# First loads on two queues, sixteen small stack copies and a re-ordered end in a two-layer attention trunk

## The chip, the cores and the metric

The kernel runs on one core of one Trainium2 chip. The metric is device time in microseconds (us) of one execution. The core has TensorE (PE), VectorE (DVE), ScalarE (ACT), GpSimd (POOL) and SyncE (SP); SP, ACT and POOL can issue DMA transfers, each on a queue of its own, in the order of their instructions.

## The reference

The input `x` has 512 tokens of width D = 2048. Two layers follow each other. Each layer is a root-mean-square norm with a gain, one input projection 2048 to 2048 (eight parts of 256), two groups of four attention heads (layer 0: dilated window and block-sparse; layer 1, heads C and D: differential and stick-breaking), a SiLU gate on each, one output projection 512 to 2048, and a residual sum. A final norm with its own gain ends it.

```python
for layer in range(DEPTH):
    h = _rmsnorm(x, norm_g[layer])
    proj = jnp.einsum('bsd,de->bse', h, w_in[layer])
    parts = jnp.split(proj, N_IN_PARTS, axis=-1)
    ...
    y = jnp.concatenate([_merge(o1) * jax.nn.silu(g1), _merge(o2) * jax.nn.silu(g2)], axis=-1)
    x = x + jnp.einsum('bse,ed->bsd', y.astype(x.dtype), w_out[layer])
return _rmsnorm(x, final_norm_g)
```

## The kernel before, in words

**Numbers in two parts.** Every operand is split into a high and a low part (`HH` and `HL`, `YH` and `YL`, `whi` and `wlo`), and a product is made of three matmuls: high by high, high by low, low by high (`mm3`). Activations are kept transposed: 16 blocks `kt` (or `dc` on the output side) of 128 channels by 512 tokens. `x` is transposed on the host.

**Weights.** Both layers' weights are 80 units of 128 x 1024 words, 512 KB each, in the order in which they are used. `load_unit` loads the next one (three `raw` buffers). `split_half` makes `whi` on ScalarE and `wlo` on VectorE or GpSimd for half a unit. `tick` is called before each half unit is used; it loads and splits ahead. All these loads are issued by SP.

**Start.** `run` clears a tile and lets PE run `WARM` products of zeros. SP then issues `xg` (block 0 of `x` and the three gains in one tensor of 560 columns), the two halves of unit 0, block 1 of `x`, unit 1, and blocks 2 to 4. In `layer` for layer 0, `make_h` multiplies a block by its gain (`HH`) and forms the rest (`HL`); for block 0 it does so on VectorE straight from `xg`. `v_unit_half` then runs the four token blocks of the value projection for one `kt`; for the first half unit it runs all four with `HH` and `whi`, then with `HL`, then with `wlo`.

**The order of the middle** is written by hand: `SCHED` gives for each step of the heads a place in PE's stream of 48 or 64 half units, and `layer` calls the steps at these places. `stack4` prepares the queries and the keys of the differential heads: it splits them into `hi` and `lo` and copies them by DMA into `st`, four blocks of 32 partitions, in which each of the four rows holds either the high or the low part. SP and POOL issue four copies each of 64 KB, and POOL then one or two more that copy rows within `st` and so wait until the first have landed. Line 446 multiplies queries by keys.

**Output projection.** `open_dc` takes a bank of the accumulator for block `dc`, and `part` adds one of the four pairs of heads. `PRE` blocks (2 in layer 0, 5 in layer 1) are begun before the last pair of heads is ready; `outproj` adds that pair, the blocks behind them are run at once. The banks are two named `acc` (in layer 1 three named `s` for blocks 2 to 4). `get_x` loads the residual block three steps ahead, in layer 1 into one of four buffers `prob`.

**End.** Layer 1 computes tokens 0 to 383 transposed, like the rest. For the last 128 tokens (`nat`, the natural layout) `last` computes the output projection in units of 256 columns, with sums of squares along the rows. For the transposed part the sums come from `nat_stats`, `replicate` spreads the norm factors over the partitions, and `scale_t` scales each block, which SP writes out. `nat_evac` adds the residual and squares a piece, `nat_sum` adds up the sums, and behind the last piece a short chain makes the last factor, with which VectorE and ScalarE scale all pieces. Before, the gain of the final norm is multiplied into each transposed block by ScalarE in `after`.

## Time and profile before

| | |
|---|---|
| time, median of 3 runs | 527.46 us (527.19 to 529.7) |
| time of the profiled execution | 527.0 us |
| its span, from the first to the last instruction | 524.9 us |
| PE busy | 511.5 us, 97% of the span |
| DVE busy | 331.8 us, 63% |
| ACT busy | 293.3 us, 56% |
| POOL busy | 180.0 us, 34% |

The profile is one execution. Its rows give the start of an instruction or of a run of equal ones, its duration, its engine and line, what it writes and reads, and in brackets how long the engine was idle before it and which engine's work ended that idle time. Matmuls are pipelined: the distance from one start to the next says what one costs, and the duration of a row is longer than that.

### The profile page before, as it was taken

The numbers are of one execution on the slowest core, as the hardware profiler recorded it, in microseconds if no ns is written. First come the engines' busy times: TensorE is split into PE (matmuls) and PEld (weight loads), VectorE is DVE, ScalarE is ACT, GpSimd is POOL, SyncE is SP. The second block draws the span as 40 slices with busy tenths as digits, with TensorE's granted clock in tenths as the row PEclk, the third lists the DMA queues.
The fourth block names the chain that finished last, engine by engine and source line by source line (L and its number), as shares of the span: only waits on it lengthen the run. The fifth ranks groups of instructions, "written<-read, shape, count | busy, mean of one in ns | idle before, by whom it ended". The sixth has DMA issues, their size and how long they took to land.

```text
span 524.9 us, 7398 instructions
## 1 busy us (share of the span) xinstructions
PE 511.5 (97%) x2505; PEld 430.7 (82%) x2505; DVE 331.8 (63%) x678; ACT 293.3 (56%) x588; POOL 180.0 (34%) x171
## 2 busy tenths in 40 slices
PE   8999999999999999999999998999999999999993
PEld 5888888888888888788888887888888888898993
DVE  5545358787786755797862872564557856784444
ACT  5477244355436554566546464743446678857843
POOL 2304353304224023377403233114520322444841
PEclk9999999999999999999999999999999999999998
DMA  8895352244314223688534274232551313156717
GB/s 306 282 401 180 120 124 93 68 117 121 120 41 121 81 80 107 204 288 302 182 121 121 80 200 123 83 119 80 146 145 71 108 54 116 62 179 208 239 70 252
DMA packets 30374, 77.65 MB, mean 148 GB/s; under 512 B 4480, under 2 KB 7424, under 8 KB 29952
## 3 DMA queue, kind: packets, MB, share of 16 engines
q1 hardware_dynamic: 27264, 70.36, 39.3%
q0 software_dynamic: 2784, 6.29, 5.5%
q10 hardware_dynamic: 288, 0.52, 0.3%
q8 instruction: 20, 0.33, 0.3%
q14 instruction: 18, 0.15, 0.1%
HBM read 61.43 MB, written 8.39 MB: 133 GB/s over the span
## 4 chain that ended last, share of the span: by engine, by line
PE 91%; DMA 3%; ACT 2%; DVE 2%; issue 1%; POOL 0%; ACTq 0%; SPq 0%; POOLq 0%
PE acc L187 17%; PE acc L189 17%; PE acc L188 17%; PE oacc L188 5%; PE oacc L189 5%; PE oacc L187 5%; PE v L187 4%; PE v L189 4%; PE v L188 4%; PE ops L509 3%; PE pt L481 3%; PE s L415 2%; DMA st<-st 1%; PE z L532 1%; PE s L446 1%
## 5 line engine op out<-in xcount | busy, mean ns | idle before, releaser
L176 POOL TENSOR_TENSOR wlo<-raw,whi 128x512 fp32r<-128x512 f32 x67 | 90.7, 1359 | 192.3 <-ACT whi L174 146.9
L187 PE MATMUL acc<-hh,whi 128*128 128x512 f32 x384 | 154.2, 402 | 0.0
L189 PE MATMUL acc<-hh,wlo 128*128 128x512 f32 x384 | 150.1, 391 | 0.0
L188 PE MATMUL acc<-hl,whi 128*128 128x512 f32 x384 | 149.7, 390 | 0.0
L174 ACT ACTIVATE whi<-raw 128x512 fp32r<-128x512 f32 x148 | 90.5, 625 | 88.7 <-issue 42.7
L189 PEld LDWEIGHTS acc<-hh,wlo 128*128 128x128 f32 x384 | 72.1, 188 | 15.6
L188 PEld LDWEIGHTS acc<-hl,whi 128*128 128x128 f32 x384 | 72.3, 188 | 12.9
L187 PEld LDWEIGHTS acc<-hh,whi 128*128 128x128 f32 x384 | 72.3, 188 | 12.7
L176 DVE TENSOR_TENSOR wlo<-raw,whi 128x512 fp32r<-128x512 f32 x81 | 59.2, 737 | 29.4 <-ACT whi L174 26.9
L187 PE MATMUL v<-whi,hh 128*128 128x512 f32 x124 | 48.4, 390 | 0.0
L189 PE MATMUL v<-whi,hl 128*128 128x512 f32 x124 | 48.3, 389 | 0.0
L188 PE MATMUL v<-wlo,hh 128*128 128x512 f32 x124 | 48.2, 389 | 0.0
L395 ACT ACTIVATE prob<-prob,m 128x512 f32<-128x512 f32 (+3 forms) x56 | 29.7, 552 | 28.3 <-DVE m L392 28.3
L487 DVE TENSOR_TENSOR pt<-pt 128x384 fp32r<-128x384 f32 (+1 forms) x48 | 27.4, 598 | 22.2 <-ACT pt L486 22.1
L486 ACT ACTIVATE pt<-pt 128x384 fp32r<-128x384 f32 (+1 forms) x48 | 23.5, 524 | 27.2 <-PE pt L481 26.9
L187 PE MATMUL oacc<-y,whi 128*128 128x512 f32 (+1 forms) x80 | 30.9, 386 | 0.1
L188 PE MATMUL oacc<-y,whi 128*128 128x512 f32 (+1 forms) x80 | 30.4, 380 | 0.2 <-DVE y L577 0.2
L189 PE MATMUL oacc<-y,wlo 128*128 128x512 f32 (+1 forms) x80 | 30.3, 378 | 0.0
L189 PEld LDWEIGHTS v<-whi,hl 128*128 128x128 f32 x124 | 23.3, 188 | 4.9
L188 PEld LDWEIGHTS v<-wlo,hh 128*128 128x128 f32 x124 | 23.3, 188 | 4.7
L187 PEld LDWEIGHTS v<-whi,hh 128*128 128x128 f32 x124 | 23.3, 188 | 4.6
L253 POOL TENSOR_TENSOR ss<-ss,sq 128x512 f32<-128x512 f32 x15 | 21.8, 1451 | 11.2 <-ACT sq L249 11.1
(219 smaller groups left out, 836.8 us busy)
## 6 DMA issues: line engine op xcount, KB each, us to landing
raw<-w SPq DMA_DIRECT2D x79, 512.0 KB, 3.4
xr<-xt SPq DMA_DIRECT2D x31, 256.0 KB, 4.4
xnat<-xnat SPq DMA_DIRECT2D x8, 512.0 KB, 7.5
x1d<-x SPq DMA_DIRECT2D x16, 256.0 KB, 2.8
xr<-x1d SPq DMA_DIRECT2D x16, 256.0 KB, 3.5
st<-st POOLq DMA_DIRECT2D x24, 128.0 KB, 3.5
out_t_dram<-x2a SPq DMA_DIRECT2D x10, 192.0 KB, 2.8
out_t_dram<-x2b SPq DMA_DIRECT2D x6, 192.0 KB, 2.5
```

The costliest lines, as they stand in the source:

```text
L174: self.nc.scalar.activation(h, t, AF.Copy)
L176: eng.tensor_tensor(l, t, h.bitcast(F32), op=OP.subtract)
L187: mm(out, lhsT=lh, rhs=rh, start=first, stop=False)
L188: mm(out, lhsT=lh, rhs=rl, start=False, stop=False)
L189: mm(out, lhsT=ll, rhs=rh, start=False, stop=last)
L253: nc.gpsimd.tensor_tensor(ss, ss, sq, op=OP.add)
L395: nc.scalar.activation(p, p, AF.Exp, bias=m[:, t:t + 1], scale=-1.0, **kw)
L415: nc.tensor.matmul(out, lhsT=Q()[:, 2 * i + arr, 128 * t:128 * t + 128], rhs=Q()[:, 4 + i, :n], start=arr == 0, stop=arr == 1)
L481: nc.tensor.transpose(bank[:, col + 128 * (t - c):col + 128 * (t - c) + 128], st["p"][:, QOFF[t] + 128 * c:QOFF[t] + 128 * c + 128], self. ...
L486: nc.scalar.activation(h, src, AF.Copy)
L487: nc.vector.tensor_tensor(l, src, h.bitcast(F32), op=OP.subtract)
L509: nc.tensor.matmul(b[:, 128 * c:], lhsT=self.V[:, c, vh], rhs=st[k][:, OFF[c]:OFF[c] + WID[c]], start=c == 0 and k == "h", stop=c == NT - ...
```

## The change

The first loads are spread over two queues and re-ordered. `xg` holds the first 256 columns of block 0, then the gains, then the other 256 columns, and is loaded in two parts; `make_h0` works on 256 columns at a time. ACT issues the first half of unit 0, and later unit 1, blocks 2 to 4 and unit 2, between its own first steps. The first half unit's products run for token blocks 0 and 1 first, then for 2 and 3. One warm-up product is left out (`WARM` 7).

In `stack4` each row of `st` is copied straight from `hi` or `lo`: eight copies by SP and eight by POOL for 512 columns of each of four blocks, none within `st`.

In the output projection blocks 2 to 4 use the banks `s` in both layers, and for blocks 0 and 1 the two products with `YH` of the last pair of heads run in front of the two with `YL`. In layer 1 the residual blocks are loaded in pairs (`get_pair`), two to a buffer, six ahead.

At the end `replicate` stands in front of the last quarter of unit 1's products, the scaling of block 0 in front of the first piece's evacuation, and the evacuation and sum of the second last piece (`nat_evac(3)`, `nat_sum(3)`) in front of the scalings of blocks 10 and 14. For blocks 0 to 4 the gain is multiplied in `scale_t` on VectorE, and ScalarE's copy in `after` goes.

```diff
@@ -37,7 +37,7 @@
...
 LEAD = [0, 16]
-WARM = 8
+WARM = 7
@@ -139,21 +139,21 @@
...
 
-    def load_unit(self, part=0):
+    def load_unit(self, part=0, eng=None):
...
         if part == 2:
-            self.nc.sync.dma_start(self.raw[0][:, 512:], self.a["w"][0][:, 512:])
+            eng.dma_start(self.raw[0][:, 512:], self.a["w"][0][:, 512:])
...
             self.raw[0] = self.wp.tile([128, 1024], F32, tag="raw", bufs=3, name="raw")
-            self.nc.sync.dma_start(self.raw[0][:, :512], self.a["w"][0][:, :512])
+            eng.dma_start(self.raw[0][:, :512], self.a["w"][0][:, :512])
...
         t = self.wp.tile([128, 1024], F32, tag="raw", bufs=3, name="raw")
-        self.nc.sync.dma_start(t, self.a["w"][u])
+        (eng or self.nc.sync).dma_start(t, self.a["w"][u])
@@ -182,11 +182,17 @@
...
 
-    def mm3(self, out, lh, ll, rh, rl, first, last):
+    def mm3(self, out, lh, ll, rh, rl, first, last, which=3):
         mm = self.nc.tensor.matmul
-        mm(out, lhsT=lh, rhs=rh, start=first, stop=False)
-        mm(out, lhsT=lh, rhs=rl, start=False, stop=False)
-        mm(out, lhsT=ll, rhs=rh, start=False, stop=last)
+        if which == 3:
+            mm(out, lhsT=lh, rhs=rh, start=first, stop=False)
+            mm(out, lhsT=lh, rhs=rl, start=False, stop=False)
+            mm(out, lhsT=ll, rhs=rh, start=False, stop=last)
+        elif which == 2:
+            mm(out, lhsT=lh, rhs=rh, start=first, stop=False)
+            mm(out, lhsT=ll, rhs=rh, start=False, stop=False)
+        else:
+            mm(out, lhsT=lh, rhs=rl, start=False, stop=last)
@@ -231,13 +237,19 @@
...
 
-    def make_h(self, x, l, kt, square=True, g=None):
-        nc = self.nc
-        if g is None:
-            g = self.g[:, l, kt:kt + 1]
-            nc.scalar.activation(self.HH[:, kt], x, AF.Copy, scale=g)
-        else:
-            nc.vector.tensor_scalar(self.HH[:, kt], x, g, None, op0=OP.mult)
+    def make_h0(self, i):
+        nc = self.nc
+        o = i * (S // 2 + 3 * KT)
+        x, g = self.xg[:, o:o + S // 2], self.xg[:, S // 2:S // 2 + 1]
+        w = slice(S // 2 * i, S // 2 * i + S // 2)
+        nc.vector.tensor_scalar(self.HH[:, 0, w], x, g, None, op0=OP.mult)
+        nc.vector.scalar_tensor_tensor(self.HL[:, 0, w], x, g, self.HH[:, 0, w].bitcast(F32),
+                                       op0=OP.mult, op1=OP.subtract)
+
+    def make_h(self, x, l, kt, square=True):
+        nc = self.nc
+        g = self.g[:, l, kt:kt + 1]
+        nc.scalar.activation(self.HH[:, kt], x, AF.Copy, scale=g)
@@ -252,12 +264,9 @@
...
 
-    def load_x(self, src, kt, tag=None):
-        if tag:
-            x = self.ap.tile([128, 1280], F32, tag=tag, bufs=4, name="xr")[:, :S]
-        else:
-            x = self.tmp("xr")
-        self.nc.sync.dma_start(x, src[kt])
+    def load_x(self, src, kt, eng=None):
+        x = self.tmp("xr")
+        (eng or self.nc.sync).dma_start(x, src[kt])
@@ -315,10 +324,10 @@
...
         if u == 0 and half == 0:
-            for x, y in ((self.HH, h), (self.HL, h), (self.HH, l)):
-                for t in range(NT):
-                    self.nc.tensor.matmul(self.vps[t], lhsT=x[:, kt, 128 * t:128 * t + 128], rhs=y[:, w],
-                                          start=x is self.HH and y is h, stop=False)
+            for x, y, t in [(x, y, t) for ts in ((0, 1), (2, 3))
+                            for x, y in ((self.HH, h), (self.HL, h), (self.HH, l)) for t in ts]:
+                self.nc.tensor.matmul(self.vps[t], lhsT=x[:, kt, 128 * t:128 * t + 128], rhs=y[:, w],
+                                      start=x is self.HH and y is h, stop=False)
@@ -370,15 +379,12 @@
...
         nc.vector.tensor_tensor(lo.bitcast(F32R), src, hi, op=OP.subtract)
+        hrows, lrows = ((0, 96), (32, 64)) if key else ((0, 64), (32, 96))
...
             p = slice(32 * i, 32 * i + 32)
-            nc.sync.dma_start(sf[0:32, z + i], hi[p])
-            nc.gpsimd.dma_start(sf[32:64, z + i], lo[p])
-        if key:
-            nc.gpsimd.dma_start(sf[64:96, z:z + 4], sf[32:64, z:z + 4])
-            nc.gpsimd.dma_start(sf[96:128, z:z + 4], sf[0:32, z:z + 4])
-        else:
-            nc.gpsimd.dma_start(sf[64:128, z:z + 4], sf[0:64, z:z + 4])
+            for k in range(2):
+                nc.sync.dma_start(sf[hrows[k]:hrows[k] + 32, z + i], hi[p])
+                nc.gpsimd.dma_start(sf[lrows[k]:lrows[k] + 32, z + i], lo[p])
@@ -615,27 +621,42 @@
...
         if k < KT:
-            self.xs[k] = self.load_x(self.px, k, "prob" if self.pl else None)
+            self.xs[k] = self.load_x(self.px, k)
+
+    def get_pair(self, k):
+        if k < KT // 2:
+            t = self.ap.tile([128, 1280], F32, tag="prob", bufs=4, name="xr")[:, :2 * S]
+            t = t.rearrange("p (k s) -> p k s", k=2)
+            self.nc.sync.dma_start(t, self.px[2 * k:2 * k + 2].rearrange("k p s -> p k s"))
+            self.xs[2 * k], self.xs[2 * k + 1] = t[:, 0], t[:, 1]
...
             for k in range(3):
-                self.get_x(k)
-        self.accs[dc] = self.bank("acc" if dc < 2 or dc >= PRE[self.pl] else "s", "oacc")[:, :self.pw]
-
-    def part(self, dc, j):
+                self.get_pair(k) if self.pl else self.get_x(k)
+        self.accs[dc] = self.bank("s" if 2 <= dc < 5 else "acc", "oacc")[:, :self.pw]
+
+    def part(self, dc, j, which=3):
...
         self.mm3(self.accs[dc], h[:, e], lo[:, e], self.YH[:, e, :self.pw], self.YL[:, e, :self.pw],
-                 j == 0, j == 3)
+                 j == 0, j == 3, which)
...
         for dc in range(KT):
-            self.get_x(dc + 3)
-            if dc < PRE[self.pl]:
+            if not self.pl:
+                self.get_x(dc + 3)
+            elif dc % 2 == 0:
+                self.get_pair(dc // 2 + 3)
+            if dc < 2:
+                if dc == 0:
+                    self.part(0, 3, 2)
+                    self.part(1, 3, 2)
+                self.part(dc, 3, 1)
+            elif dc < PRE[self.pl]:
@@ -660,7 +681,8 @@
...
                 nc.scalar.activation(sq[:, :TW], X[dc], AF.Square)
-            nc.scalar.activation(X[dc], X[dc], AF.Copy, scale=self.g[:, 2, dc:dc + 1])
+            if dc >= PRE[1]:
+                nc.scalar.activation(X[dc], X[dc], AF.Copy, scale=self.g[:, 2, dc:dc + 1])
@@ -702,7 +724,10 @@
...
             for dc in dcs:
-                eng.tensor_tensor(X[dc], X[dc], r, op=OP.mult)
+                if dc < PRE[1]:
+                    eng.scalar_tensor_tensor(X[dc], X[dc], self.g[:, 2, dc:dc + 1], r, op0=OP.mult, op1=OP.mult)
+                else:
+                    eng.tensor_tensor(X[dc], X[dc], r, op=OP.mult)
@@ -753,12 +778,14 @@
...
         nat_mm(nb[:, :256], [0], (3,))
-        nat_mm(nb[:, 256:], [1])
+        nat_mm(nb[:, 256:], [1], (0, 1, 2))
         self.replicate(3)
+        nat_mm(nb[:, 256:], [1], (3,))
+        scale_t([11, 12], nc.gpsimd, False)
+        scale_t([0], nc.vector)
...
         nat_sum(0)
-        scale_t([11, 12], nc.gpsimd, False)
-        scale_t([0, 1, 2], nc.vector)
+        scale_t([1, 2], nc.vector)
@@ -779,9 +806,9 @@
...
         nat_mm(nb[:, :256], [6])
-        scale_t([10, 14], nc.vector)
...
         nat_sum(3)
+        scale_t([10, 14], nc.vector)
@@ -814,10 +841,17 @@
...
                 if kt == 0:
-                    self.make_h(self.x0.pop(0), 0, 0, False, self.xg[:, S:S + 1])
+                    q = self.nc.scalar
+                    self.make_h0(0)
                     self.split_half()
+                    self.load_unit(0, q)
+                    self.x0[2] = self.load_x(self.a["xt"], 2, q)
+                    self.make_h0(1)
...
                     self.make_h(self.x0.pop(1), 0, 1, False)
+                    for k in (3, 4):
+                        self.x0[k] = self.load_x(self.a["xt"], k, q)
+                    self.load_unit(0, q)
@@ -938,16 +972,14 @@
...
         self.xg = self.ap.tile([128, 1280], F32, tag="prob", bufs=4, name="xg")[:, :S + 3 * KT]
-        nc.sync.dma_start(self.xg, self.a["xg"])
-        self.x0[0] = self.xg[:, :S]
+        c = S // 2 + 3 * KT
+        nc.sync.dma_start(self.xg[:, :c], self.a["xg"][:, :c])
+        self.load_unit(1, nc.scalar)
+        nc.sync.dma_start(self.xg[:, c:], self.a["xg"][:, c:])
         nc.scalar.preload_act_table_set("exp_and_others")
-        self.load_unit(1)
-        self.load_unit(2)
+        self.load_unit(2, nc.sync)
         self.x0[1] = self.load_x(self.a["xt"], 1)
-        nc.gpsimd.tensor_copy(self.g.rearrange("p a b -> p (a b)"), self.xg[:, S:])
-        self.load_unit()
-        for kt in range(2, 5):
-            self.x0[kt] = self.load_x(self.a["xt"], kt)
+        nc.gpsimd.tensor_copy(self.g.rearrange("p a b -> p (a b)"), self.xg[:, S // 2:c])
@@ -1048,7 +1080,8 @@
...
     g = np.stack([norm_g[0], norm_g[1], final_norm_g])
-    ins["xg"] = np.concatenate([ins["xt"][0], g.reshape(3, KT, 128).transpose(2, 0, 1).reshape(128, 3 * KT)], axis=1)
+    gc = g.reshape(3, KT, 128).transpose(2, 0, 1).reshape(128, 3 * KT)
+    ins["xg"] = np.concatenate([ins["xt"][0][:, :S // 2], gc, ins["xt"][0][:, S // 2:]], axis=1)
```

## Rows read from the trace of the kernel before

**Rows 1.** The page, part 1: busy time, share of the span, instructions

```profile
PE 511.5 (97%) x2505; PEld 430.7 (82%) x2505; DVE 331.8 (63%) x678; ACT 293.3 (56%) x588; POOL 180.0 (34%) x171
```

**Rows 2.** Waits of PE: total us, times, longest us

```profile
PE s L446 <- DMA st<-st: 1.6, 1, 1.6
...
PE xnp L678 <- DMA xr<-x1d: 0.9, 1, 0.9
PE v L320 <- ACT whi L174: 0.6, 1, 0.6
PE oacc L188 <- DVE y L577: 0.2, 1, 0.2
```

**Rows 3.** Timeline, 0 to 16 us: start us, us, engine, line

```profile
1.19 3.48 PE L938 MATMUL warm<-zero 128*128 128x512 bf16 x8 [1.19 <-DVE zero L935]
...
2.60 0.43 SPq L156 DMA_DIRECT2D raw<-w  x1
...
4.57 0.63 ACT L174 ACTIVATE whi<-raw 128x512 fp32r<-128x512 f32 x1 [2.55 <-DMA raw<-w]
...
5.25 1.19 PE L320 MATMUL v<-whi,hh 128*128 128x512 f32 x4 [0.58 <-ACT whi L174]
...
7.39 0.75 DVE L241 SCALAR_TENSOR_TENSOR hl<-xr,gcols,hh 128x512 fp32r<-128x512 f32 x1 [0.35 <-ACT hh L238]
...
8.56 0.39 PE L189 MATMUL v<-whi,hl 128*128 128x512 f32 x1
...
10.83 0.39 PE L187 MATMUL v<-whi,hh 128*128 128x512 f32 x1
```

**Rows 4.** Stretches: us; busy PE, PEld, DVE, ACT, POOL; clock, DMA, GB/s

```profile
5.25:8.00 2.75, 2.75 (x12) 2.29 (x13) 1.98 (x3) 1.36 (x2) 0.00 (x0) 1.00 1.03 390
...
215.00:257.00 42.00, 41.91 (x185) 34.31 (x184) 35.58 (x41) 28.05 (x47) 28.52 (x20) 1.00 0.74 260
```

**Rows 5.** Timeline of PE, 213 to 217 us

```profile
213.98 0.51 PE L187 MATMUL oacc<-y,whi 128*128 128x512 f32 x1
214.70 0.50 PE L188 MATMUL oacc<-y,whi 128*128 128x512 f32 x1 [0.22 <-DVE y L577]
...
215.74 0.39 PE L189 MATMUL oacc<-y,wlo 128*128 128x512 f32 x1
...
216.21 0.50 PE L187 MATMUL oacc<-y,whi 128*128 128x512 f32 x1
```

**Rows 6.** Timeline of SP's and POOL's queues, 300 to 345 us

```profile
308.67 2.78 SPq L375 DMA_DIRECT2D st<-hi  x4
...
309.66 1.98 POOL L376 DMA_DIRECT2D st<-lo  x4 [1.96 <-DVE lo L372]
```

**Rows 7.** The chain that ended last, 275 to 478 us

```profile
311.14 3.21 DMA st<-lo
...
314.91 0.09 POOL st L378
...
315.49 7.18 DMA st<-st
...
475.43 2.60 DMA xr<-x1d
```

**Rows 8.** Timeline, 513 to 517 us

```profile
513.97 0.28 PE L189 MATMUL nacc<-wkh,y 128*128 128x256 f32 x1
...
514.39 1.01 DVE L705 TENSOR_TENSOR x2b<-x2b,rep 128x384 f32<-128x384 f32 x2
...
515.32 0.42 DVE L715 TENSOR_TENSOR nat<-nacc,nat 128x256 f32<-128x256 f32 x1
...
515.83 0.42 ACT L717 ACTIVATE sqn<-nat 128x256 f32<-128x256 f32 x1 [1.14 <-DVE nat L715]
515.85 0.28 PE L189 MATMUL xnp<-wkh,y 128*128 128x256 f32 x1
...
516.80 0.37 ACT L792 ACTIVATE sqn<-xnp 128x256 f32<-128x256 f32 x1
```

**Rows 9.** Instructions on the blocks x2a: duration ns min/median/max, first and last start

```profile
L663 ACT ACTIVATE x2a<-x2a,gcols x10: 614/618/620, 476.0 to 491.0; 128x384 f32<-128x384 f32 x10
```

## The prediction

> **What bounds the kernel now.** The page comes first: PE is busy for 511.5 us of a span of 524.9 us [rows 1]. A shorter kernel must therefore close gaps in PE's stream or shorten what stands before its first and behind its last product; work saved on the other engines counts only where PE waits for it. The list of PE's waits has four entries inside the stream [rows 2]: 1.6 us for a stacked operand of layer 1, 0.9 us for a residual tile in the last projection, 0.6 us for the first split weight, 0.2 us for a `YL` in layer 0. The reader should then go to the places. A wait costs more than its idle time, because the pipeline must fill again, so I take start-to-start distances of matmuls where I have them. Behind PE's last product the span still holds a chain over VectorE and ScalarE; that end is read by itself, below.
>
> The sums go against the profiled execution: span 524.9 us, time 527.0 us, so 2.1 us lie around the span. The median of the three runs is 527.46 us, 0.46 us above it; I subtract from the median.
>
> **Start.** The first product starts at 5.25 us, right behind the first half split, whose data were there at 4.57 us [rows 3]. Before, one SP queue carries `xg` (128 x 560 words, 287 KB) and then the half unit (262 KB). After, the half unit has ACT's queue, and only the first 304 columns of `xg` (156 KB) can go ahead of it. That is 131 KB less; at the 390 GB/s of the window just behind [rows 4] it is 0.34 us, so the first product moves to about 4.9 us. The new order (token blocks 0 and 1, then 2 and 3) lets PE begin when half of `HH` is there; the VectorE order has each second operand ready before its product: three operands of 256 columns cost about half the 0.75 us of 512 [rows 3].
>
> How far can it move? The next operand in need is `HL` of `kt` = 1: it is ready at 7.39 + 0.75 = 8.14 us and used at 8.56 us [rows 3], a slack of 0.42 us, and the bytes in front of its `x1` are the same as before. Unit 1 was issued at 2.60 us and serves from 10.83 us [rows 3]; it and `x2` are now issued by ACT behind the first split, at about 4.9 and 5.3 us. At 390 GB/s the 786 KB of both need 2.0 us. What a load takes beyond its transfer I estimate from a lone one: 262 KB landed 2.60 us after the issue [rows 7], 1.9 us more than 0.67 us at that rate. So both are there at 4.9 + 1.9 + 2.0 = 8.8 us, and `HH` and `HL` of `kt` = 2, about 0.7 us each, follow at some 10.3 us. That cover is thin, 0.5 us less what PE gains. I take a gain of 0.3 us; bounds +0.4 (then `x1` binds) and -1.9 (unit 1 is later by its whole delay in issue, 4.9 - 2.6 = 2.3 us, with 0.4 of it hidden).
>
> The Trainium skill, page "DMA: Bandwidth & Descriptors", section "Rules for kernel authors", says that spreading transfers over issuing engines brings no bandwidth, since the queues share the same engines and interleave, and saves issue time alone. By it `xg`'s second part shares the time of the half unit, and the start term could shrink to nothing; the sum would be 0.3 us less. The 390 GB/s that one queue already reaches in [rows 4] agrees with that rule, and I have therefore counted bytes ahead and not a second queue's rate.
>
> One warm-up matmul less: eight took 3.48 us, 0.435 us each for 512 columns, the 1.2 GHz level [rows 3]. Between 8.56 and 10.83 us ten products take 2.27 us, 0.23 us each: the 2.4 GHz level. The warm stretch now ends at about 4.24 us, where PE has nothing to do anyway, so I price it at nothing; if the level rises late, each product until then costs 0.2 us more (rival below).
>
> **Layer 0, output projection.** In [rows 5] the second product of the last part of `dc` 0 waits for `YL`: 0.72 us from start to start against 0.23 us; then `dc` 2 waits for the bank of `dc` 0: 0.47 us. Each is followed by a first step of about 0.34 us. The lost time is 0.49 + 0.24 us and 0.11 us of refilling twice, 0.95 us. After, four products that need only `YH` stand in front (213.98, then 0.23 us apart), so that the first with `YL` would start at 214.90 us, later than the 214.70 us at which it could start before; and `dc` 2 to 4 have three banks of their own. Both waits go: 0.95 us. The cover behind it: from 215 to 257 us VectorE is busy 35.58 of 42 us [rows 4], the fullest stretch of the kernel, so a PE that is a microsecond ahead here could run into late splits. Lower bound 0.
>
> **`stack4`.** Today the last four small copies are issued by POOL from 309.66 us, two larger copies wait for their landing, and the second of these lands 7.18 us after 315.49 us, at 322.67 us; PE stands 1.6 us idle [rows 2, 6, 7]. After, all sixteen small copies start from `hi` and `lo`. POOL issues eight at 1.98 / 4 = 0.5 us, until 313.7 us; SP eight at 2.78 / 4 = 0.7 us, from 308.67 until 314.2 us [rows 6]. The landing of the last small one was waited for 3.21 us after its issue [rows 7]: about 317.4 us. PE needs them at 322.67 - 1.6, about 321 us. Even if a small copy took the 7.18 us it would be there at 321.4 us. I take the whole wait, 1.6 us, plus 0.1 us of refill: 1.7 us; lower bound 1.2 us by the slow landing. SP's queue holds the next weight load 2.8 us longer, and POOL's its next split; POOL, however, no longer stands in front of the larger copies until 314.9 us [rows 7].
>
> The same page of the Trainium skill and section advise to coalesce small transfers, because those under 64 KB are mostly overhead. That speaks against this edit, which makes 64 KB pieces out of a 256 KB copy. The rows decide otherwise here: the coalesced copy cannot start before the small ones have landed, and it is that chain of two landings which PE waits for. If the pieces are slow, the term is 1.2 us and not 1.7 us.
>
> **Residual tiles in pairs.** Tile 4 of layer 1 is issued at 475.43 us, when the first of four buffers comes free, and lands 2.60 us later [rows 7]; PE waits 0.9 us [rows 2]. After, a buffer holds two tiles: tiles 0 to 5 are asked for when the projection opens, before 466 us, and 6 and 7 soon after. Later pairs wait for the same releases as before, at the same distance (tile 8 for the release of tile 1, with six steps to spare). The wait goes, 0.9 us plus 0.1 us of refill: 1.0 us; lower bound 0.5 us, since a pair is a transfer twice as long and the first five steps use tiles quickly.
>
> **End.** VectorE's evacuation of the second last piece starts at 515.32 us, behind the scalings of 10 and 14 which begin at 514.39 us; ScalarE's squares follow at 515.83 us, its sums, and then the squares of the last piece at 516.80 us [rows 8]. The piece itself has been complete since 513.97 + 0.28 = 514.25 us. After, the evacuation starts at 514.39 us, 0.93 us earlier, and ScalarE would be free at 516.80 - 0.93 = 515.87 us. Then PE binds: 516.13 us plus some 0.06 us of signalling. The gain is 516.80 - 516.19 = 0.6 us; bounds 0.2 us (if the moved scalings or their outgoing DMAs delay the last steps) and 0.9 us. The moved `replicate`, the gain of `dc` 0 to 4 in the scaling and the five copies on ScalarE that go (0.62 us each [rows 9]) I price at nothing: a `scalar_tensor_tensor` costs 0.75 x 384 / 512 = 0.56 us by [rows 3] against 0.50 us (1.01 / 2 [rows 8]), five times 0.06 = 0.3 us of VectorE; it hides under the PE products of the next piece, and with that cover gone would cost those 0.3 us.
>
> **Sum.** 0.3 + 0.95 + 1.7 + 1.0 + 0.6 = 4.55 us. 527.46 - 4.55 = 522.9 us, that is 0.86% less. What a measurement of this kernel can tell from no change is about 0.5%, 2.6 us: faster means under 524.8 us, slower over 530.1 us. With all lower bounds the gain is -1.9 + 0 + 1.2 + 0.5 + 0.2 = 0, with the upper ones 0.4 + 0.95 + 1.7 + 1.0 + 0.9 = 5.0 us.
>
> **Rivals.**
> 1. A closed wait opens again further on. PE runs up to 3 us ahead of today's times, and where VectorE is 85% busy [rows 4] a split or an evacuation becomes late. For: that stretch. Against: in [rows 2] PE has no wait there, and the helpers are started by PE's own progress, so most shift with it. Price: the layer 0 term, and the stack term at its lower bound, 0.95 + 0.5 = 1.45 us; time 524.4 us.
> 2. The loads on ACT's queue come late: unit 1, `x2`, and behind them `x3`, `x4` and unit 2, which stand behind a ScalarE step that itself waits for `x1`. For: the issue moves from 2.60 to 4.9 us while SP's later loads compete. Against: the 8.8 us worked out above. Price 2.2 us against my start term: 522.9 + 2.2 = 525.1 us, the same. The whole becomes slower only if each of the five loads in turn stops PE and the first 17 us lose more than 4.6 + 2.6 = 7.2 us; with five stalls of 2.0 us the time is 522.9 + 0.3 + 10 = 533.2 us.
> 3. The clock rises later. If PE needs as long a stretch of real products at the low level as the warm one was, 3.48 us, eight products cost 0.2 us more each: 1.6 us, 524.5 us. For: one warm matmul less and a gap before the first product. Against: in the trace of before the rise came without the gap doing harm.
>
> **Chances.** Forecast 0.62 (its own range 521.9 to 523.9 us); rival 1 0.16; rival 2 0.11 for the mild form and 0.04 for the slow one; rival 3 0.07. Faster: 0.62 + 0.16 + 0.07 = 0.85; same 0.11; slower 0.04. The range 521.7 to 525.2 us holds the forecast, rivals 1 and 3 and most of the mild rival 2.
>
> **What would show it.** The first product at about 4.9 us, and no PE wait from there to 30 us; no `s` wait for `st`, no `xnp` wait for `xr`, no step over 0.3 us in the first two `dc` of layer 0; the last squares at PE's end. PE's wait list should then hold hardly more than the first product. The prediction is wrong if PE shows new waits for `hl`, `whi` or `wlo`, or if a landing of `st` is still the last thing before `s`.

## Result and profile after

The changed kernel takes 523.33 us (median of 4 runs, 522.92 to 524.28) where the kernel before takes 527.91 us beside it (4 runs, 527.19 to 529.7). The ratio is 0.991, interval 0.9888 to 0.9931: faster by 0.9%. The forecast was 522.9 us, in a range from 521.7 to 525.2 us. The profiled execution took 523.6 us with a span of 521.4 us; the one before had 527.0 and 524.9 us, so these two traces differ by 3.5 us of span and the medians by 4.6 us.

The page of the kernel after, and below it the list of PE's waits (waited in total, times, longest), answer to [rows 1] and [rows 2]:

```profile
PE 511.5 (98%) x2504; PEld 431.1 (83%) x2504; DVE 335.3 (64%) x680; ACT 290.1 (56%) x583; POOL 187.3 (36%) x181
```

```profile
PE warm L972 <- DVE zero L969: 1.2, 1, 1.2
PE v L189 <- POOL wlo L176: 0.3, 1, 0.3
PE v L329 <- ACT whi L174: 0.3, 1, 0.3
```

PE is busy as long as before, to a tenth; what went is idle time. None of the waits for `st`, `xr` and `YL` is left. One wait is new: a `wlo` by POOL in the value projection. Now the places, each by a timeline of the kernel after (start, duration, engine and line, in brackets the idle time before it).

**The start** lost 1.0 us in this execution instead of gaining:

```profile
4.62 1.22 PE L329 MATMUL v<-whi,hh 128*128 128x512 f32 x2 [0.26 <-ACT whi L174]
6.21 0.63 PE L329 MATMUL v<-wlo,hh 128*128 128x512 f32 x2
7.46 0.44 ACTq L156 DMA_DIRECT2D raw<-w  x1
8.05 0.39 PE L188 MATMUL v<-whi,hh 128*128 128x512 f32 x1
...
15.00 0.63 ACT L174 ACTIVATE whi<-raw 128x512 fp32r<-128x512 f32 x1 [3.40 <-DMA raw<-w]
15.71 1.29 POOL L176 TENSOR_TENSOR wlo<-raw,whi 128x512 fp32r<-128x512 f32 x1 [4.02 <-ACT whi L174]
16.30 0.49 PE L188 MATMUL v<-whi,hh 128*128 128x512 f32 x1
17.05 0.50 PE L189 MATMUL v<-wlo,hh 128*128 128x512 f32 x1 [0.26 <-POOL wlo L176]
17.60 0.50 PE L190 MATMUL v<-whi,hl 128*128 128x512 f32 x1
...
22.73 0.39 PE L188 MATMUL v<-whi,hh 128*128 128x512 f32 x1
```

The last line is the first product of `kt` = 6, behind all stalls of the start. The same product in the kernel before:

```profile
21.71 0.39 PE L187 MATMUL v<-whi,hh 128*128 128x512 f32 x1
```

The first product starts 0.63 us earlier than in [rows 3] (4.62 for 5.25 us), and `kt` = 1 only 0.06 us earlier (8.05 us; before it was 8.11 us). The first four products take 1.59 us (4.62 to 6.21 us) where the 2.4 GHz level gives 4 x 0.23 = 0.92 us; in experiment 3, where they run at that level and the first step refills the pipeline, they take 1.04 us. The granted clock in the profile's rows reads 1.00 all through the start, also for the warm-up products that stand 0.43 us apart, so the level is read here from the distances alone. Then `kt` = 4 meets the split of unit 2: ACT issued its load at 7.46 us, sat idle for 3.40 us until the data were there, and split it at 15.00 us. PE's steps from 16.30 over 17.05 and 17.60 to 17.94 us lose 0.52 + 0.32 + 0.11 us against 0.23 us a step.

**Layer 0, output projection**, beside [rows 5]:

```profile
215.00 0.50 PE L192 MATMUL oacc<-y,whi 128*128 128x512 f32 x1
215.34 0.40 PE L193 MATMUL oacc<-y,wlo 128*128 128x512 f32 x1
...
216.03 0.62 PE L195 MATMUL oacc<-y,whi 128*128 128x512 f32 x2
216.49 0.39 PE L188 MATMUL oacc<-y,whi 128*128 128x512 f32 x1
```

The one step over 0.23 us is 215.00 to 215.34 us. Block 2 starts 0.46 us behind the last two products of block 1, without a wait for a bank.

**The stack**, beside [rows 6, 7]: the two issuing queues, and the line on landings of the tile `st` between 305 and 324 us:

```profile
308.77 5.50 SPq L386 DMA_DIRECT2D st<-hi  x8
309.76 3.91 POOL L387 DMA_DIRECT2D st<-lo  x8 [3.52 <-DVE lo L381]
```

```profile
DMA to landing us min/median/max: 1.9/2.8/3.4
```

The last copy is issued by about 314.3 us, none takes over 3.4 us, so all are there by 317.7 us (the prediction said 317.4), and PE starts its products of `st` at 321.38 us.

**The cover behind layer 0**, the window that answers to [rows 4] (columns: stretch, us, PE, PEld, DVE, ACT and POOL busy with instructions, granted clock, DMA share, GB/s):

```profile
215.00:257.00 42.00, 42.00 (x186) 34.81 (x186) 38.02 (x42) 27.28 (x46) 30.13 (x20) 1.00 0.74 259
```

VectorE is still fuller than before, 38.02 of 42 us for 35.58 us, and PE has no gap in it.

**The end**, beside [rows 8]:

```profile
511.12 0.28 PE L190 MATMUL nacc<-wkh,y 128*128 128x256 f32 x1
511.55 0.41 DVE L740 TENSOR_TENSOR nat<-nacc,nat 128x256 f32<-128x256 f32 x1
511.88 1.47 DVE L730 TENSOR_TENSOR x2b<-x2b,rep 128x384 f32<-128x384 f32 x3
512.05 0.42 ACT L742 ACTIVATE sqn<-nat 128x256 f32<-128x256 f32 x1 [0.21 <-DVE nat L740]
513.00 0.28 PE L190 MATMUL xnp<-wkh,y 128*128 128x256 f32 x1
513.38 0.38 ACT L819 ACTIVATE sqn<-xnp 128x256 f32<-128x256 f32 x1 [0.25 <-PE xnp L190]
```

The evacuation of the second last piece stands directly behind that piece's last product and in front of the scalings; the last squares now wait for PE and start 0.1 us behind its end (513.28 us). Before, PE had been done for 0.67 us when they started [rows 8].

### The profile page after: what moved, and what is told of

Read it like the earlier page. It is cut to its first block, busy times and chain, and to the rows that moved or that the text cites. A ratio compares the mean times of both kernels' runs of the same rounds, so it can differ in the third digit from the quotient of the medians.

```text
span 521.4 us, 7398 instructions
## 1 busy us (share of the span) xinstructions
PE 511.5 (98%) x2504; PEld 431.1 (83%) x2504; DVE 335.3 (64%) x680; ACT 290.1 (56%) x583; POOL 187.3 (36%) x181
## 3 DMA queue, kind: packets, MB, share of 16 engines
q0 software_dynamic: 2944, 5.25, 4.5%
## 4 chain that ended last, share of the span: by engine, by line
PE 95%; DMA 3%; ACT 1%; SPq 0%; DVE 0%; ACTq 0%; issue 0%
PE acc L188 17%; PE acc L190 17%; PE acc L189 17%; PE v L190 5%; PE v L188 5%; PE v L189 5%; PE oacc L188 5%; PE oacc L190 5%; PE oacc L189 5%; PE ops L515 4%; PE pt L487 3%; PE s L421 2%; DMA raw<-w 1%; PE z L538 1%; PE s L452 1%; DMA xr<-xt 1%
## 5 line engine op out<-in xcount | busy, mean ns | idle before, releaser
L188 PE MATMUL acc<-hh,whi 128*128 128x512 f32 x384 | 154.2, 402 | 0.0
L188 PEld LDWEIGHTS acc<-hh,whi 128*128 128x128 f32 x384 | 72.3, 188 | 12.7
L176 DVE TENSOR_TENSOR wlo<-raw,whi 128x512 fp32r<-128x512 f32 x81 | 61.5, 765 | 29.3 <-ACT whi L174 28.6
L188 PE MATMUL v<-whi,hh 128*128 128x512 f32 x124 | 48.5, 391 | 0.0
L188 PE MATMUL oacc<-y,whi 128*128 128x512 f32 (+1 forms) x76 | 29.1, 383 | 0.0
L190 PE MATMUL oacc<-y,wlo 128*128 128x512 f32 (+1 forms) x76 | 28.8, 379 | 0.0
L189 PE MATMUL oacc<-y,whi 128*128 128x512 f32 (+1 forms) x76 | 28.8, 379 | 0.0
L188 PEld LDWEIGHTS v<-whi,hh 128*128 128x128 f32 x124 | 23.3, 188 | 4.9 <-ACT hh L252 0.3
L265 POOL TENSOR_TENSOR ss<-ss,sq 128x512 f32<-128x512 f32 x15 | 23.5, 1568 | 8.7 <-ACT sq L261 8.5
```

Source lines behind the costliest of these rows:

```text
L176: eng.tensor_tensor(l, t, h.bitcast(F32), op=OP.subtract)
L188: mm(out, lhsT=lh, rhs=rh, start=first, stop=False)
L189: mm(out, lhsT=lh, rhs=rl, start=False, stop=False)
L190: mm(out, lhsT=ll, rhs=rh, start=False, stop=last)
L265: nc.gpsimd.tensor_tensor(ss, ss, sq, op=OP.add)
```

## Experiments

Each kernel still computes the whole reference. Times are medians of the runs with their spread; each ratio is against the kernel before on the same chip. That kernel takes 527.03 to 527.45 us beside the experiments and 527.91 us beside the changed kernel, which was not run again; so a difference of half a microsecond between an experiment and the changed kernel's 523.33 us tells nothing by itself.

**1. The start as before**, everything else as after: one transfer for `xg`, all loads by SP in the old order, eight warm-up products, `make_h0` on 512 columns, the old order of the first products.

```diff
-WARM = 7
+WARM = 8
-        self.load_unit(1, nc.scalar)
+        self.load_unit(1, nc.sync)
...
+        self.load_unit()
+        for kt in range(2, 5):
+            self.x0[kt] = self.load_x(self.a["xt"], kt)
```

> The kernel after, with the start of before (one queue for the first loads, xg in one piece, products over all four token blocks, 8 warm-up products); all else as after. Theory A, the new start costs about 1 us (the products of half unit 4 wait for a late unit 2, and the first products run at the lower clock): no PE wait between 6 and 30 us, the last accumulation of layer 0 at about 207.7 to 208.4 us instead of 209.4, and a time about 1.0 us under the kernel after, 522.3 us. Theory B, the new start gains the 0.3 us that was forecast and the wait at 17 us is an accident of one execution: about 523.6 us.

Measured: 523.08 us (522.89 to 523.38, 5 runs), ratio 0.9918 [0.9904, 0.9932]. That is 0.25 us less than the changed kernel's 523.33 us, less than the spreads tell apart. It lies between the two theories and settles neither: by time the start as a whole can't be told from nothing. Its profile is no clean old start, either. From PE's waits there:

```profile
PE v L188 <- ACT hh L251: 0.4, 1, 0.4
```

It is `HH` of `kt` = 1, for which [rows 2] show no wait. The old order has stalls of its own in some executions.

The traces say more of the start than the times. The first product of `kt` = 6 begins at 21.71, 22.38, 22.43 and 21.66 us in the profiled executions with the old start (the kernel before, experiments 1, 10 and 11), and at 22.73, 23.62, 22.35, 22.12 and 22.23 us in those with the new start as it stands (the changed kernel, experiments 5 to 8). The means are 22.05 and 22.61 us. That points to a cost of half a microsecond and not to a gain; the two groups overlap, so it is not shown.

**2. Unit 2 ahead of blocks 3 and 4** on ACT's queue:

```diff
                     self.x0[2] = self.load_x(self.a["xt"], 2, q)
+                    self.load_unit(0, q)
...
                         self.x0[k] = self.load_x(self.a["xt"], k, q)
-                    self.load_unit(0, q)
```

> The kernel after, with unit 2 issued by ACT right behind x2, in front of x3 and x4. Theory A: unit 2 lands by 12 us instead of 15.0, the wait for its low part at 17 us (0.53 + 0.32 + 0.11 us) goes, and the time falls by 0.5 to 1.0 us to about 522.6 us; x3 lands up to 1.4 us later and has about 0.9 us of cover, so a wait of up to 0.5 us for HH or HL of kt 3 at 13.5 us may take its place. Theory B, the wait stems from the competition of SP's loads and not from the place of unit 2 in ACT's order: unit 2 still lands after 14 us, time as the kernel after.

Measured: 523.2 us (522.96 to 523.6, 6 runs), ratio 0.9919 [0.9905, 0.9933]. The split of unit 2 starts at 13.91 us instead of 15.00 us, not by 12 us, and PE has no wait there. But ACT now idles for block 3:

```profile
13.28 0.72 ACT L252 ACTIVATE hh<-xr,gcols 128x512 fp32r<-128x512 f32 x1 [2.11 <-DMA xr<-xt]
14.05 0.19 PEld L188 LDWEIGHTS v<-whi,hh 128*128 128x128 f32 x1 [0.42 <-ACT hh L252]
```

`kt` = 6, behind all stalls of the start, begins at 22.68 us, in the changed kernel at 22.73 us. The wait has only moved.

**3 and 4. Eight and ten warm-up products** instead of seven, `WARM = 8` and `WARM = 10`, each alone.

> The kernel after, with 8 warm-up products as before instead of 7. If the low clock of the first four products (0.59, 0.42, 0.36 us apart) comes from the missing warm-up product, they are 0.23 to 0.3 us apart and the products of kt 1 can start up to 0.5 us earlier than 8.05 us, unless HL of kt 1 (ready at 8.09 us) holds them. If it comes from the earlier start alone, the first two or three products are still slow and kt 1 starts at about 8.05 us. Time within 0.5 us of the kernel after in both cases.

> The kernel after, with 10 warm-up products: these end at about 5.3 us, so the first real product starts at about 5.3 us instead of 4.6, at the higher clock. If the clock is what the early start lost, kt 1 starts at about 8.05 us as in the kernel after: nothing lost although the first product is 0.7 us later. If the clock does not matter, kt 1 starts 0.7 us later, at 8.7 us. The wait at 17 us stays or shrinks by the same amount.

Measured: 523.96 us (523.11 to 524.86, 4 runs), 0.9934 [0.9916, 0.9953] for eight; 523.82 us (523.47 to 524.57, 4 runs), 0.9933 [0.9917, 0.995] for ten. Neither is better than seven by time. With eight, the first products ran at the high level in the profiled execution (four in 1.04 us), so PE reached `kt` = 1 at 7.64 us, 0.4 us earlier than with seven, and then stood longer at `kt` = 4, from 15.75 to 17.13 us and again to 17.87 us:

```profile
4.79 0.73 PE L329 MATMUL v<-whi,hh 128*128 128x512 f32 x2 [0.19 <-ACT whi L174]
5.83 0.62 PE L329 MATMUL v<-wlo,hh 128*128 128x512 f32 x2
...
15.75 0.39 PE L190 MATMUL v<-whi,hl 128*128 128x512 f32 x1
15.83 0.63 ACT L174 ACTIVATE whi<-raw 128x512 fp32r<-128x512 f32 x1 [3.08 <-DMA raw<-w]
17.13 0.50 PE L188 MATMUL v<-whi,hh 128*128 128x512 f32 x1 [0.99 <-ACT hh L252]
17.87 0.50 PE L189 MATMUL v<-wlo,hh 128*128 128x512 f32 x1 [0.24 <-POOL wlo L176]
```

With ten, the real products follow the warm ones without a gap, and the first two steps were still slow: 1.21 us from 5.08 to 6.29 us, a part of it behind the last warm product. It reached `kt` = 1 at 8.62 us, near the 8.7 us of the second case, and PE then had no wait at all; `kt` = 6 began at 22.22 us.

```profile
5.08 1.39 PE L329 MATMUL v<-whi,hh 128*128 128x512 f32 x2
6.29 0.65 PE L329 MATMUL v<-whi,hl 128*128 128x512 f32 x2
```

So in experiment 3 the earlier PE paid it back at `kt` = 4, and in neither did more warm products fix when the high level begins.

**5. `stack4` as before**, the rest as after: four copies each from `hi` and `lo`, then copies within `st`.

```diff
-            for k in range(2):
-                nc.sync.dma_start(sf[hrows[k]:hrows[k] + 32, z + i], hi[p])
-                nc.gpsimd.dma_start(sf[lrows[k]:lrows[k] + 32, z + i], lo[p])
+            nc.sync.dma_start(sf[0:32, z + i], hi[p])
+            nc.gpsimd.dma_start(sf[32:64, z + i], lo[p])
+        if key:
+            nc.gpsimd.dma_start(sf[64:96, z:z + 4], sf[32:64, z:z + 4])
+            nc.gpsimd.dma_start(sf[96:128, z:z + 4], sf[0:32, z:z + 4])
...
```

> The kernel after, with stack4 as before (small copies and then the larger ones within st). If the chain of two landings is what PE waited for, PE waits again for st in front of s near 320 us, 1.6 us idle and 1.75 us from start to start, and the time is about 1.7 us over the kernel after, 525.0 us. If the closed wait only moved, PE waits elsewhere less and the time rises by under 0.8 us.

Measured: 524.75 us (523.3 to 524.8, 4 runs), 0.9934 [0.9911, 0.9957]. The profiled execution shows no wait for `st` at all; the last landing came early enough:

```profile
316.02 0.49 POOL L388 DMA_DIRECT2D st<-st  x1
322.29 0.79 PE L455 MATMUL s<-st 128*128 128x512 f32 x4
```

and from the view of the tile `st` between 305 and 324 us:

```profile
DMA to landing us min/median/max: 2.5/2.9/4.8
```

The last copy, issued at 316.02 us, took at most 4.8 us, so it was there by 320.8 us; in [rows 7] it took 7.18 us. Even at the changed kernel's 321.38 us PE would not have waited for it. Of the 1.3 us by which this span is longer than the changed kernel's (522.7 and 521.4 us), 0.9 us were lost in the start (`kt` = 6 at 23.62 for 22.73 us; `PE v L188` waits 0.8 us for an `hh` there). This run's time can therefore not price the edit; experiments 10 and 11 do.

**6. Residual tiles one by one**, as before, four buffers.

```diff
-                self.get_pair(k) if self.pl else self.get_x(k)
+                self.get_x(k)
...
-            if not self.pl:
-                self.get_x(dc + 3)
-            elif dc % 2 == 0:
-                self.get_pair(dc // 2 + 3)
+            self.get_x(dc + 3)
```

> The kernel after, with residual blocks of layer 1 loaded one by one, three ahead. If the four buffers were the cause, PE waits again for xr at dc 4, near 475 us, 0.9 us idle and 1.0 us from start to start; time about 1.0 us over the kernel after, 524.3 us. If the wait would be hidden anyway: no PE wait there, same time.

Measured: 524.69 us (524.15 to 524.93, 4 runs), 0.9938 [0.9918, 0.9958], 1.4 us more than the changed kernel's median. The wait is back where it was; a timeline of this kernel:

```profile
474.86 0.33 PE L190 MATMUL oacc<-y,wkl 128*128 128x384 f32 x1
476.36 0.30 PE L702 MATMUL xnp<-ident,xr 128*128 128x128 f32 x1 [1.17 <-DMA xr<-x1d]
```

From 474.86 to 476.36 us are 1.50 us for a step of 0.17 us (473.42 to 473.59 us for the same kind): 1.33 us.

**7. Banks as before**: in layer 0 blocks 2 to 4 use `acc` again; the order of the `YH` and `YL` products stays.

```diff
-        self.accs[dc] = self.bank("s" if 2 <= dc < 5 else "acc", "oacc")[:, :self.pw]
+        self.accs[dc] = self.bank("s" if 2 <= dc < PRE[self.pl] else "acc", "oacc")[:, :self.pw]
```

> The kernel after, with the accumulator banks of before in layer 0 (blocks 2 to 4 on the two acc banks); the new order of the YH products stays. If the bank was a wait of its own, the first product of dc 2 is 0.4 to 0.5 us behind its predecessor instead of 0.23 (loss 0.25 to 0.35 us), perhaps more because the evacuation of dc 0 now starts two products later. If the wait for YL was the whole cause, dc 2 starts on time and the time is that of the kernel after.

Measured: 523.81 us (523.69 to 525.91, 5 runs), 0.9933 [0.9912, 0.9954]. A timeline shows the wait for the bank, longer than before:

```profile
215.42 0.62 PE L195 MATMUL oacc<-y,whi 128*128 128x512 f32 x2
215.84 1.29 DVE L990 TENSOR_TENSOR x<-oacc,xr 128x512 f32<-128x512 f32 x2 [0.79 <-PE oacc L195]
216.59 0.50 PE L188 MATMUL oacc<-y,whi 128*128 128x512 f32 x1 [0.55 <-DVE x L990]
```

From 215.42 to 216.59 us are 1.17 us for two products (0.46 us): 0.71 us, and 0.10 us of refill behind it (the next product at 216.92 us). Before, the bank cost 0.24 + 0.11 us. The re-ordered products finish block 0 later, so its evacuation starts later: the order needs the banks. Without them it closes 0.60 us (`YL`) and opens 0.46 us. The banks with the old order were not run.

**8. The second last piece behind the scalings again**; `replicate`, the gains and the rest of the end as after.

```diff
+        scale_t([10, 14], nc.vector)
...
         nat_sum(3)
-        scale_t([10, 14], nc.vector)
```

> The kernel after, with the scalings of blocks 10 and 14 in front of the second last piece's evacuation and sum again. Forecast step: that order alone delays the last squares by 0.6 us, from PE's end to 0.6 us behind it; time 0.6 us over the kernel after, 523.9 us. Rival: the end gained by the other moves (replicate, gain folded in), and the squares start as in the kernel after.

Measured: 523.83 us (523.46 to 525.47, 5 runs), 0.9935 [0.9908, 0.9963]. By time it can't be told from the changed kernel; by the place it can:

```profile
512.39 0.42 ACT L742 ACTIVATE sqn<-nat 128x256 f32<-128x256 f32 x1 [1.14 <-DVE nat L740]
513.37 0.37 ACT L819 ACTIVATE sqn<-xnp 128x256 f32<-128x256 f32 x1
```

The last squares follow ACT's sums without idle time, at 513.37 us, 11.91 us behind PE's last `ssp` product (501.46 us); in the changed kernel it is 513.38 - 502.06 = 11.32 us, and in the kernel before 516.80 - 504.86 = 11.94 us. The order alone carries the 0.6 us. The moved `replicate` and the gains on VectorE, which this kernel keeps, carry nothing that shows at this place.

**9. All loads but the first half unit by SP**, in the old order, with the divided `xg` and seven warm-up products.

```diff
                     self.make_h0(0)
-                    self.load_unit(0, q)
-                    self.x0[2] = self.load_x(self.a["xt"], 2, q)
...
-                    self.load_unit(0, q)
+        self.load_unit()
+        for kt in range(2, 5):
+            self.x0[kt] = self.load_x(self.a["xt"], kt)
```

> The kernel after, with ACT issuing the first half of unit 0 alone; unit 1, x2 to x4 and unit 2 are issued by SP behind x1, in the order of before. Theory A, the start's early gain is lost because ACT issues unit 2 late (its split began at 14.3 to 15.9 us in five executions with the new start, at 11.4 and 12.1 us with the old one): the split of unit 2 begins by 12 us, PE has no wait at 16 to 18 us, the first product stays at about 4.6 us, half unit 6 starts at 21.2 to 21.8 us instead of 22.1 to 23.6, and the time falls by about 0.8 us to 522.5 us. Theory B, the bytes needed in the first 16 us bind whatever the order: the waits move to kt 1 to 3, half unit 6 starts at 22.3 us or later, time as the kernel after, 523.3 us.

Measured: 523.67 us (522.92 to 524.27, 6 runs), 0.9926 [0.9898, 0.9954]. The split of unit 2 starts at 12.64 us and waits for PE, no longer for its data, and PE has no wait behind the first product. Yet the profiled execution lost as much as that wait had cost by the low level, and `kt` = 6 began at 23.32 us:

```profile
5.91 1.05 PE L329 MATMUL v<-whi,hl 128*128 128x512 f32 x2
...
8.47 0.93 PE L329 MATMUL v<-whi,hl 128*128 128x512 f32 x2
...
12.64 0.63 ACT L174 ACTIVATE whi<-raw 128x512 fp32r<-128x512 f32 x1 [1.55 <-PE v L190]
```

Six products from 5.91 to 8.47 us take 2.56 us, 0.43 us each, the distance of the 1.2 GHz level; from 8.9 us on they take 0.23 us. The row of that stretch reads a granted clock of 1.00 (the number behind POOL's), so the profile does not confirm the level:

```profile
5.91:8.47 2.56, 2.56 (x7) 1.98 (x6) 1.54 (x3) 1.35 (x2) 0.00 (x0) 1.00 0.98 373
```

The time is that of theory B, but the waits that theory B wants at `kt` = 1 to 3 did not come.

**10. The new `stack4` alone** in the kernel before: the diff of `stack4` as it stands in the change, and nothing else.

> The kernel before with the new stack4 alone. Theory A, the chain of two landings costs what the profile of before shows in every execution: no PE wait for st, time 1.7 us under the kernel before, about 525.7 us. Theory B, the landing of the last larger copy varies (7.18 us in that profile, under 6.3 us where stack4 was put back and PE did not wait) and the term is mostly smaller than its one reading: 0 to 1.0 us under before, 526.5 to 527.4 us.

Measured: 525.88 us (524.93 to 528.5, 12 runs) beside 527.03 us (525.82 to 530.69, 17 runs), ratio 0.9976 [0.9957, 0.9994]. In its list of PE's waits none is for `st`, while those for `xr` (0.8 us) and `YL` (0.2 us) stand. The edit gives 1.15 us by the medians, with an interval of 0.3 to 2.3 us (0.06% to 0.43%).

**11. The kernel before once more**, for its waits in another execution.

> The kernel before once more, for a second profile of it. Theory A: PE waits again about 1.6 us for st near 321 us, the last larger copy lands 7 us after its issue. Theory B: it lands in 5 to 6 us and PE waits under 0.5 us. In both, the waits of layer 0's projection (0.5 and 0.25 us) and of dc 4 in layer 1 (1.0 to 1.3 us) come again, since they follow from buffers and order.

Measured: 526.56 us, span 524.5 us. PE's waits:

```profile
PE xnp L678 <- DMA xr<-x1d: 1.4, 2, 0.9
PE s L446 <- DMA st<-st: 0.5, 1, 0.5
```

and in the chain that ended last:

```profile
315.63 5.85 DMA st<-st
```

The same copy, issued 0.14 us later than in [rows 7], landed after 5.85 us and not 7.18 us; the wait is 0.5 us and not 1.6 us. The residual tiles wait twice here, 1.4 us in all, not once for 0.9 us. `YL` costs 0.2 us of waiting in both.

**12. Experiment 9 with nine warm-up products**, the best of the starts put together.

```diff
-WARM = 7
+WARM = 9
```

> The kernel after with the later loads on SP (as in the run before this one) and 9 warm-up products, so that the warm-up ends at about 5.0 us, where the first real product can start: no gap between them. Theory A, the gap of 0.5 to 1 us before the first real product is what lets the clock rise late (in the profile without the extra two products eleven real products were 0.43 us apart, until 8.9 us): the real products are 0.23 us apart from 5.5 us on, kt 1 starts by 8.3 us, half unit 6 by 22.0 us, and the time is 522.5 to 523.0 us. Theory B, the rise comes at a time that differs from execution to execution whatever PE did just before: several real products are 0.43 us apart again in this profile or not, by chance, and the time is 523.3 to 523.9 us, like the run before.

Measured: 522.95 us (522.72 to 523.94, 6 runs), ratio 0.993 [0.9913, 0.9948], span 520.9 us, PE without any wait behind the warm products. It is the lowest median of all, 0.4 us under the changed kernel and 0.1 us under experiment 1; the runs overlap, and its ratio is no lower than theirs (0.991 and 0.9918), so it is not shown to be faster than either. The high level came late here as well, though the real products follow the warm ones without a gap; four products take 1.99 us, a part of it behind the last warm product:

```profile
4.66 1.42 PE L329 MATMUL v<-whi,hh 128*128 128x512 f32 x2
6.65 0.62 PE L329 MATMUL v<-wlo,hh 128*128 128x512 f32 x2
```

The time is that of theory A, the products are those of theory B: a gap in front of the real products is not needed for the high level to come late.

## Why the prediction was right, step by step

The total was right: 4.55 us forecast, 4.58 us measured by the medians of one comparison (527.91 - 523.33). That they agree to 0.03 us is luck: the interval of the ratio reaches from 3.6 to 5.9 us, and within the sum two terms were mis-sized, both too high.

- **Layer 0, 0.95 us: right.** Of the 0.49 + 0.24 + 2 x 0.11 us lost, one refill of 0.11 us stayed, so 0.84 us. Experiment 7 shows that the banks are needed for it.
- **`stack4`, 1.7 us: the mechanism right, the size not.** No landing stands in front of `s` any more, and the small copies landed as forecast, within 3.4 us. The term took one execution's wait for the kernel's. The wait was 1.6 us there, 0.5 us in experiment 11, and absent in experiment 5. By itself the edit gave 1.15 us (0.3 to 2.3 us); the lower bound of 1.2 us was nearer, but for another reason than the one given for it, a small copy that lands late. In the profiled pair it is worth the full 1.75 us, because the profiled execution of before had the slow landing. The advice of the Trainium skill that weighed against this edit ("DMA: Bandwidth & Descriptors", "Rules for kernel authors", to coalesce small transfers) did not bear out here: pieces of 64 KB landed in 1.9 to 3.4 us, the 256 KB copy in up to 4.8 us, 5.85 us and 7.18 us, each time behind a wait for the first.
- **Residual pairs, 1.0 us: right**, rather low: 1.33 us at the place in experiment 6 (1.4 us by the time), and the kernel before has a second such wait in some executions.
- **End, 0.6 us: right**, and for the reason given: PE now binds the last squares. The edits priced at nothing are worth nothing (experiment 8).
- **Start, +0.3 us: the step that failed.** By the medians it can't be told from nothing (experiment 1); in the profiled pair it is -1.0 us, and -0.6 us by the means of the traces (not shown beyond their scatter), within the bounds of -1.9 and +0.4 us. The sign that the prediction named for being wrong, a new wait for `wlo`, came here. The step reads "that cover is thin" and was worked out for unit 1 and `x2`. These came in time: ACT split unit 1 at 8.40 us, about as the 8.8 us said. The load that came late was unit 2, which ACT issued at 7.46 us behind blocks 3 and 4 and which I had not worked out in the sum; it stood in rival 2 only. Putting it first moved the wait to block 3 (experiment 2). Giving everything but the half unit back to SP's queue took the wait away (experiments 9 and 12). The early first product, for its part, was eaten by the low level, as in rival 3, though for four products and not eight: they cost 0.55 us more than in experiment 3.

Of the rivals, the mild form of 2 and a part of 3 happened together, for about 1 us in the profiled pair. There the parts add up to -1.0 + 0.84 + 1.75 + 1.0 + 0.6 = 3.2 of 3.5 us of span, not to 4.55 us. The medians give 1.1 us more and hide the loss, since the profiled execution of before lay 0.9 us under the median of its comparison and that of after 0.3 us above. Rival 1 did not happen: PE ran through the fullest stretch without a gap.

Where the start is left out, the terms can be read without its scatter. From the first product of `kt` = 6 to the end of the span the kernel before takes 503.2 us (524.9 - 21.7) and 502.8 us in experiment 11, the changed kernel 498.7 us. Experiments 1, 2, 3, 9 and 12, which change the start alone, take 498.6 to 498.8 us and experiment 4 499.3 us. So everything behind the start gave 4.2 to 4.5 us, where the prediction's other four terms add up to 4.25 us. Put back one at a time, the pairs cost 1.4 us (500.05 us in experiment 6), the banks 0.8 us (499.48 us in experiment 7) and the end 0.5 us (499.17 us in experiment 8), though a scatter like experiment 4's is as large as the last.

The Trainium skill's rule that queues share the same engines ("DMA: Bandwidth & Descriptors", "Rules for kernel authors") fits a start that gained nothing; but what the runs show beside it is that the order on a second queue decides who is late.

**What stays open.** What sets the moment at which the high level begins was not found; the number of warm-up products did not set it in these runs. Nor is the best order of the first loads found: experiments 1, 9 and 12 and the changed kernel are within 0.8 us, and their runs overlap. Where the remaining 0.3 us of the span came from was not followed.

## What to carry to other kernels

A wait for a DMA landing in one trace is one draw: before its full length goes into a sum, look at the same wait in a second execution, or take it at the shorter landing. When loads are re-ordered, work out the arrival of every load until the stream is in steady state, the last one on the new queue above all, since here a start that gained 0.63 us at the first product gave it back, and more, at an operand that came later than before. And when the order of products is changed so that an operand may come later, ask which bank is freed later by it: the two edits in layer 0 were worth 0.84 us together, and the order alone would have gained 0.60 - 0.46 = 0.14 us.

## What the runs showed of the hardware

- The moment at which products change from 0.43 to 0.23 us, the distances of the 1.2 and 2.4 GHz levels, varied from execution to execution: before 4.6 us in experiment 5 and at about 5.9 us in the changed kernel, both with seven warm products, 6.3 us with ten, 6.6 us with nine, 8.9 us with seven again (experiment 9). It did not follow the number of warm products. The profile's granted clock reads 1.00 at either distance.
- The same 256 KB copy within `st`, issued at 315.49, 315.63 and 316.02 us, took 7.18, 5.85 and at most 4.8 us to land (the kernel before, experiments 11 and 5).
- A unit of 512 KB issued on ACT's queue at 7.46 us, with blocks 3 and 4 ahead of it and SP's queue loading beside it, was split at 15.00 us, 7.5 us behind its issue; a residual tile of 262 KB landed 2.60 us behind its issue [rows 7].
